# Four output tiles computed together, h tile by h tile, behind each norm; GpSimd taken out of the norms, ScalarE scales the residual

## The chip, the cores and the metric

One core of a Trainium2 chip runs the whole program in one launch. The metric is the device time of that launch in microseconds (us); the kernel before took 3902.36 us, the median of three runs (3899.41 to 3907.14). TensorE (PE) multiplies matrices, VectorE (DVE), ScalarE (ACT) and GpSimd (POOL) work element by element, and SyncE (SP) issues the transfers. Each engine executes its own queue in order and waits at semaphores for the others.

## The reference, cut to what matters

One sequence of 512 tokens with 1024 features passes through a first block (attention and a state-space layer, then a gated FFN, with RMS norms) and then through four layers of a second block. Layer i takes a mixer (0 a conformer convolution module, 1 HGRN2, 2 mLSTM, 3 stick-breaking attention) and then a convolutional FFN. Everything around the change is in these lines:

```
for i in range(4):
    h = x * (1 + scale1) + shift1
    y = mixer_i(h)
    x = layer_norm(ALPHA * x + (1 + gate1) * y, g0, b0)
    h = x * (1 + scale2) + shift2
    y = conv_ffn(h)                  # up: 1024 -> 2 x 2816, conv, silu(gate) * val, down
    x = layer_norm(ALPHA * x + (1 + gate2) * y, g1, b1)
```

A norm needs, for each token, the mean and the mean square over all 1024 features. Two affine copies of the normalized x are used afterwards: h, the input of the next matrix product, and x again as the residual (already multiplied by ALPHA).

## The kernel before

**Layout.** Features lie on partitions: X is eight tiles of 128 features by 512 tokens, and so is h. For precision each float32 operand of a product is split into a high part (a cast to fp32r) and a low part (the difference), so that one 128x128 weight block times one h tile is three matmuls: `mm3` issues L251 (high weight, high h), L254 (low weight, high h) and L255 (high weight, low h). An output tile is a sum over eight h tiles, 24 matmuls into one PSUM bank.

**Weights.** `wload` transfers a block, casts it on ACT (L236) and subtracts on DVE (L237). Four high and four low weight buffers exist, which is just what four output tiles need; a buffer can be cast again once PE's last matmul with it is done.

**Halves.** Around a norm the 512 tokens are worked in two halves of 256 (`HALF`), so that one half can be normalized while PE works on the other. `feats` loops over the halves and in each over four output tiles (`feat`, one bank each, from the four banks of `psm`); `down4` does the last four tiles of a projection in this way. Behind every tile the residual is added on DVE (L624, `add_res`), and `stat` squares the new X on ACT (L343) and adds value and square to running sums on POOL (L356, L358; in the conformer on DVE). With the last tile of a half, float32 matmuls with a matrix of 1/1024 (L348 and L349 for the mean, L351 and L352 for the mean square) give the sums over all partitions in two banks of `psa`.

**The norm.** `ln_scale` forms the variance and its inverse root (ACT L384, three DVE steps L385 to L387 that refine it), subtracts the mean from eight tiles (DVE L399) and multiplies them (L410: six on DVE, tiles 3 and 6, `POOLK`, on POOL). Subtractions 4 to 7 all come ahead of the first multiplication. `ln_apply` then makes hf from X (ACT L444, for tiles 3 and 6 POOL L439), its high part (ACT L244 or L441) and its low part (DVE L247 or POOL L442), and at the end scales X itself for the residual, on POOL (L453), in each half.

**Order.** The Python program is traced in order; a planner then orders each engine's queue by its own estimate of when each instruction can start, earlier program lines first among those that are ready. So a queue need not follow the program, and once the program is built its order is fixed. `tc.add_manual_dep` (`after`) pins an order by hand.

**Where the next stage starts.** Behind the norms stand: the first four up-projection tiles of each FFN (`up` with `jb == 0`, in halves), the first four of HGRN2 (`dense` with `hp == 0`), of mLSTM and of the conformer, and the conformer's own inner norm with `proj_res(early=True)`. The stick layer uses `tok_steps` instead. In the FFN and in mLSTM a tile's bank is read by ACT (L328, `conv_taps`) and by one DVE instruction per tap (L667). In the conformer the first products go through a gate (L1318) into a convolution of 31 taps, done for each of eight tiles partly as DVE steps (L1300) and partly as matmuls (L1294 to L1296).

Of the kernel before, what the change touches and what calls it, by code (L numbers as in the profile page):

```python
# [12 lines left out]
AF = mybir.ActivationFunctionType  # L13
# [17 lines left out]
POOLK = (3, 6)  # L31
# [56 lines left out]
class Kern:  # L88
# [248 lines left out]
    def stat(self, i, v, q, part):  # L337
# [6 lines left out]
        if i == self.ntot - 1:  # L344
# [44 lines left out]

    def ln_scale(self, o, w, X, pool=POOLK):  # L390

# [14 lines left out]
        for k in (4, 5, 6, 7):  # L406
            self.after(sub(k), self.newton)
        for k in range(8):
            e = nc.gpsimd if k in pool else nc.vector
            e.tensor_tensor(out=X[k][:, c], in0=X[k][:, c], in1=y, op=ALU.mult)  # L410
# [14 lines left out]
    def ln_apply(self, gx, bx, gh, bh, parts=HALF):  # L425
# [5 lines left out]
        for o, w in parts:  # L431
            c = slice(o, o + w)
            self.ln_scale(o, w, X, POOLK if gh is not None else ())
            last = None
            for k in range(8) if gh is not None else ():
                hf = self.tmp("hf")[:, :w]
                hi, lo = self.Hh[k][:, c], self.Hl[k][:, c]
                if k in POOLK:
                    nc.gpsimd.tensor_scalar(out=hf, in0=X[k][:, c], scalar1=gh[:, k:k + 1], scalar2=bh[:, k:k + 1],  # L439
                                            op0=ALU.mult, op1=ALU.add)  # L440
                    nc.scalar.copy(out=hi, in_=hf)  # L441
                    last = nc.gpsimd.tensor_tensor(out=lo, in0=hf, in1=hi, op=ALU.subtract)  # L442
                else:
                    nc.scalar.activation(out=hf, in_=X[k][:, c], func=AF.Identity, scale=gh[:, k:k + 1],  # L444
                                         bias=bh[:, k:k + 1])
                    self.split(hf, hi, lo)
            for k in range(8):
                x = X[k][:, c]
                if last is None and k % 2:
                    nc.scalar.activation(out=x, in_=x, func=AF.Identity, scale=gx[:, k:k + 1], bias=bx[:, k:k + 1])  # L450
                    continue
                e = nc.vector if last is None else nc.gpsimd
                i = e.tensor_scalar(out=x, in0=x, scalar1=gx[:, k:k + 1], scalar2=bx[:, k:k + 1], op0=ALU.mult,  # L453
                                            op1=ALU.add)
                if last is not None:
                    self.after(i, last)
# [1678 lines left out]
```

## Time and profile before

| what | value |
|---|---|
| median of three runs | 3902.36 us |
| the profiled execution: own time, span | 3907.43 us, 3905.7 us |
| TensorE clock granted over the span | 0.971 of full |
| busy: PE, DVE, ACT, POOL | 3749.0, 2596.6, 2078.7, 1380.1 us |
| chain that ended last | PE 74%, DVE 11%, POOL 6%, DMA 3%, ACT 3%, issue 2% |
| transferred | 458.06 MB, mean 117 GB/s |

An engine counts as busy while at least one of its instructions runs. The ends of matmuls are modelled and overlap, so that a PE that is only trickling still looks busy; the number of matmuls in a stretch, times the interval at which they start when nothing hinders them, tells how much of the stretch PE needed.

### The profile page before, as it was taken

What the parts mean: (1) busy time and instruction counts of PE and PEld (TensorE: products, weight loads), DVE (VectorE), ACT (ScalarE), POOL (GpSimd) and SP (SyncE); (2) the same over time, 40 slices, a digit from 0 to 9 for tenths busy, and PEclk for the clock granted to TensorE, in tenths of its full rate; (3) what the DMA queues carried; (4) which work ended last, traced back from release to release, by engine and by line L of the source; (5) the groups of instructions that cost most, each with busy time, mean ns of one, the idle gap of its engine ahead of it and who ended that gap; (6) DMA issues with size and microseconds to landing.
All of it is one profiled execution on the core that took longest, in us unless ns stands there. A gap on an engine that the chain in (4) does not pass through costs nothing.

```text
span 3905.7 us, 51250 instructions
## 1 busy us (share of the span) xinstructions
PE 3749.0 (96%) x19014; PEld 3048.5 (78%) x19014; DVE 2596.6 (66%) x3960; ACT 2078.7 (53%) x3757; POOL 1380.1 (35%) x1358
## 2 busy tenths in 40 slices
PE   8999999999996999999999999999899999999998
PEld 7665678878876887898888888776777878788887
DVE  5678866665698765676676567457776566676545
ACT  4555664564644654476465446654556445554333
POOL 5567602343002543342454341255734340022000
PEclk9898899999998999999999999999999999999999
DMA  4111243555321454332245535342255531132231
GB/s 150 54 57 44 69 143 120 190 168 170 108 87 34 157 189 155 122 101 78 99 151 191 166 100 173 133 134 78 74 185 171 173 108 61 46 106 82 93 106 66
DMA packets 393431, 458.06 MB, mean 117 GB/s; under 512 B 35571, under 2 KB 307357, under 8 KB 393181
## 3 DMA queue, kind: packets, MB, share of 16 engines
q1 hardware_dynamic: 393181, 454.78, 35.9%
q8 instruction: 150, 2.46, 0.3%
q14 instruction: 100, 0.82, 0.1%
HBM read 421.56 MB, written 33.03 MB: 116 GB/s over the span
## 4 chain that ended last, share of the span: by engine, by line
PE 74%; DVE 11%; POOL 6%; DMA 3%; ACT 3%; issue 2%; SPq 0%; DVEq 0%; POOLq 0%; ACTq 0%
PE bank L251 20%; PE bank L254 20%; PE bank L255 20%; DMA mix<-in_ada_w_dram 3%; DVE wl L237 2%; PE bank L1906 1%; POOL mix L585 1%; DVE cacc L1300 1%; PE bank L1071 1%; PE bank L1914 1%; ACT mix L583 1%; PE bank L317 1%; PE bank L319 1%; PE bank L318 1%; PE bank L874 1%
## 5 line engine op out<-in xcount | busy, mean ns | idle before, releaser
L251 PE MATMUL bank<-hh,wh 128*128 128x512 f32 (+1 forms) x2928 | 1101.0, 377 | 12.5 <-ACT hh L244 5.3
L254 PE MATMUL bank<-hh,wl 128*128 128x512 f32 (+1 forms) x2928 | 1095.0, 375 | 4.1 <-DVE wl L237 4.1
L255 PE MATMUL bank<-hl,wh 128*128 128x512 f32 (+1 forms) x2928 | 1090.0, 376 | 4.0 <-DVE hl L247 3.4
L237 DVE TENSOR_TENSOR wl<-raw,wh 128x1024 fp32r<-128x1024 f32 (+2 forms) x524 | 668.6, 1277 | 205.9 <-ACT wh L236 199.7
L236 ACT CAST wh<-raw 128x1024 fp32r<-128x1024 f32 (+1 forms) x550 | 562.5, 1026 | 390.9 <-PE bank L255 338.2
L585 POOL TENSOR_TENSOR mix<-mix,mix 128x512 f32<-128x512 f32 x336 | 501.3, 1492 | 757.1 <-ACT mix L583 740.2
L251 PEld LDWEIGHTS bank<-hh,wh 128*128 128x128 f32 x2928 | 557.4, 190 | 126.5 <-ACT hh L244 8.7
L254 PEld LDWEIGHTS bank<-hh,wl 128*128 128x128 f32 x2928 | 556.8, 190 | 111.4 <-DVE wl L237 6.8
L255 PEld LDWEIGHTS bank<-hl,wh 128*128 128x128 f32 x2928 | 551.8, 190 | 114.6 <-DVE hl L247 4.5
L583 ACT ACTIVATE mix<-mix,cs 128x512 f32<-128x512 f32 x384 | 270.6, 722 | 296.9 <-DMA mix<-in_ada_w_dram 295.4
L667 DVE SCALAR_TENSOR_TENSOR mix<-bank,vl,mix 128x510 f32<-128x510 f32 (+3 forms) x384 | 268.6, 700 | 205.2 <-ACT mix L328 197.1
L254 PE MATMUL bank<-uh,wl 128*128 128x512 f32 (+1 forms) x1008 | 371.0, 368 | 3.6 <-DVE wl L237 3.6
L251 PE MATMUL bank<-uh,wh 128*128 128x512 f32 (+1 forms) x1008 | 370.5, 368 | 0.0
L255 PE MATMUL bank<-ul,wh 128*128 128x512 f32 (+1 forms) x1008 | 369.9, 367 | 0.0
L624 DVE SCALAR_TENSOR_TENSOR X<-bank,M,X 128x512 f32<-128x512 f32 (+1 forms) x192 | 120.6, 635 | 238.5 <-PE bank L255 238.2
L254 PEld LDWEIGHTS bank<-uh,wl 128*128 128x128 f32 x1008 | 189.5, 188 | 39.4 <-DVE wl L237 5.4
L251 PEld LDWEIGHTS bank<-uh,wh 128*128 128x128 f32 x1008 | 189.5, 188 | 35.1
L255 PEld LDWEIGHTS bank<-ul,wh 128*128 128x128 f32 x1008 | 189.5, 188 | 34.1
L328 ACT ACTIVATE mix<-bank,vl 128x512 f32<-128x512 f32 (+1 forms) x192 | 141.1, 735 | 86.3 <-PE bank L255 86.2
L244 ACT CAST uh<-mix 128x512 fp32r<-128x512 f32 x110 | 68.0, 618 | 174.3 <-DVE mix L694 173.9
L247 DVE TENSOR_TENSOR ul<-mix,uh 128x512 fp32r<-128x512 f32 x110 | 95.8, 871 | 75.6 <-ACT uh L244 75.1
L358 POOL TENSOR_TENSOR qs<-qs,sq 128x256 f32<-128x256 f32 (+1 forms) x88 | 106.7, 1214 | 54.1 <-ACT sq L343 53.5
(810 smaller groups left out, 7067.1 us busy)
## 6 DMA issues: line engine op xcount, KB each, us to landing
mix<-in_ada_w_dram SPq DMA_DIRECT2D x384, 256.0 KB
raw<-in_ffn_w_up_dram SPq DMA_DIRECT2D x88, 1024.0 KB
raw<-in_ffn_w_down_dram SPq DMA_DIRECT2D x32, 1024.0 KB
raw<-in_w_in_dram SPq DMA_DIRECT2D x22, 1024.0 KB
raw<-in_w_up_dram SPq DMA_DIRECT2D x22, 1024.0 KB
raw<-in_hg_w_in_dram SPq DMA_DIRECT2D x16, 1024.0 KB
raw<-in_ml_w_up_dram SPq DMA_DIRECT2D x16, 1024.0 KB
raw<-in_cc_w_pw_dram SPq DMA_DIRECT2D x12, 1024.0 KB
```

What stands on the lines that cost most here:

```text
L236: nc.scalar.copy(out=h, in_=src)
L237: eng.tensor_tensor(out=l, in0=src, in1=h, op=ALU.subtract)
L247: nc.vector.tensor_tensor(out=lo, in0=src, in1=hi, op=ALU.subtract)
L251: i = mm(out=out, lhsT=wh, rhs=xh, start=start, stop=False)
L254: mm(out=out, lhsT=wl, rhs=xh, start=False, stop=False)
L255: return mm(out=out, lhsT=wh, rhs=xl, start=False, stop=stop)
L328: self.nc.scalar.activation(out=dst[:, o:o + w], in_=ps, func=func, **kw)
L358: self.qadd.tensor_tensor(out=self.qs[:, c], in0=self.qs[:, c], in1=q[:, c], op=ALU.add)
L583: nc.scalar.activation(out=o, in_=o, func=AF.Copy, scale=self.cs[:, k:k + 1])
L585: nc.gpsimd.tensor_tensor(out=acc, in0=acc, in1=o, op=ALU.add)
L624: self.nc.vector.scalar_tensor_tensor(out=x, in0=ps, scalar=gate[:, n:n + 1], in1=x, op0=ALU.mult, op1=ALU.add)
L667: nc.vector.scalar_tensor_tensor(out=d, in0=ps[:, :n - s], scalar=col(s), in1=d, op0=ALU.mult, op1=ALU.add)
```

## The change

`feats` gets `by_k`: four banks are taken at once, the loop over h tiles is outside and the loop over the four output tiles inside, and only then is `use` called for the four. In the second half the banks come from `psa` (banks 4 to 7) if that ring has more than three banks, else from `psm` again (mLSTM). It is used behind the norms, in the conformer's projection, and in the conformer's first block, there with all 512 tokens at a time (before: halves). HGRN2's change of banks moves behind its first `dense`.

`stat` gets `direct`: in the second half of `down4` the last four tiles are not added to the running sums but multiplied by the 1/1024 matrix themselves, one matmul each for value and square as it comes.

In `ln_scale` all multiplications are on DVE, each of tiles 4 to 7 directly behind its subtraction, and `use(k)` follows each; `ln_apply` makes hf on ACT for all eight tiles and scales X on ACT, eight instructions of 512 tokens, behind both halves.

```diff
-    def stat(self, i, v, q, part):
+    def stat(self, i, v, q, part, direct=False):
...
-        if i == self.ntot - 1:
+        if direct:
+            if i == self.ntot - 4:
+                self.st[o] = tuple(self.psa()[:, 0:w] if x else None for x in (self.wmean, True))
+            for ps, t, x in zip(self.st[o], (self.vs if self.wmean else None, self.qs), (v, q)):
+                if ps is None:
+                    continue
+                if i == self.ntot - 4:
+                    mm(out=ps, lhsT=self.smat, rhs=t[:, c], start=True, stop=False)
+                mm(out=ps, lhsT=self.smat, rhs=x[:, c], start=False, stop=i == self.ntot - 1)
+        elif i == self.ntot - 1:
...
-        for k in (4, 5, 6, 7):
-            self.after(sub(k), self.newton)
         for k in range(8):
-            e = nc.gpsimd if k in pool else nc.vector
-            e.tensor_tensor(out=X[k][:, c], in0=X[k][:, c], in1=y, op=ALU.mult)
+            if k >= 4:
+                self.after(sub(k), self.newton)
+            nc.vector.tensor_tensor(out=X[k][:, c], in0=X[k][:, c], in1=y, op=ALU.mult)
+            if use is not None:
+                use(k)
...
-            self.ln_scale(o, w, X, POOLK if gh is not None else ())
...
+            def use(k):
                 hf = self.tmp("hf")[:, :w]
...
+                nc.scalar.activation(out=hf, in_=X[k][:, c], func=AF.Identity, scale=gh[:, k:k + 1], bias=bh[:, k:k + 1])
+                self.set_h(k, c, hf)
+
+            self.ln_scale(o, w, X, use if gh is not None else None)
+        for k in range(8):
+            nc.scalar.activation(out=X[k], in_=X[k], func=AF.Identity, scale=gx[:, k:k + 1], bias=bx[:, k:k + 1])
...
-    def feats(self, tiles, xh, xl, use, halves):
+    def feats(self, tiles, xh, xl, use, halves, by_k=False):
...
-        for parts in (((p,) for p in HALF) if halves else (FULL,)):
+        for p, parts in enumerate(((p,) for p in HALF) if halves else (FULL,)):
+            if by_k:
+                (o, w), = parts
+                get = self.psa if p and len(self.bank["ax"].t) > 3 else self.psm
+                banks = [get()[:, 0:w] for _ in tiles]
+                for k in range(8):
+                    for ps, (blk, j) in zip(banks, tiles):
+                        wh, wl = blk[0][2][j]
+                        self.mm3(ps, wh[:, k, :], wl[:, k, :], xh[k][:, o:o + w], xl[k][:, o:o + w], k == 0, k == 7)
+                for i, ps in enumerate(banks):
+                    use(i, (ps, o, w))
+                continue
...
-            self.stat(*ts[i], part[1:])
+            self.stat(*ts[i], part[1:], direct=part[1] > 0)
...
-        K.feats([(b, jj) for jj in range(2) for b in (bg, ba)], K.Hh, K.Hl, use, jb in (0, 3))
+        K.feats([(b, jj) for jj in range(2) for b in (bg, ba)], K.Hh, K.Hl, use, jb == 3, jb == 0)
```

## Rows read from the trace of the kernel before

**Rows 1.** The page's first part: busy us (share of the span) xinstructions.

```profile
PE 3749.0 (96%) x19014; PEld 3048.5 (78%) x19014; DVE 2596.6 (66%) x3960; ACT 2078.7 (53%) x3757; POOL 1380.1 (35%) x1358
```

**Rows 2.** Stretches: window, us, busy by engine (xcount), clock, DMA share, GB/s; seven norms.

```profile
1262.00:1285.00 23.00, 18.80 (x122) 16.45 (x123) 21.55 (x44) 17.64 (x44) 17.08 (x23) 0.93 0.46 156
1644.00:1668.00 24.00, 21.81 (x145) 19.91 (x144) 23.69 (x55) 14.95 (x33) 19.07 (x25) 0.86 0.30 91
1935.70:1958.00 22.30, 18.19 (x115) 15.63 (x115) 21.54 (x44) 16.47 (x41) 16.69 (x22) 0.90 0.45 154
2314.00:2345.00 31.00, 26.75 (x192) 24.22 (x191) 28.23 (x58) 19.99 (x51) 24.78 (x30) 0.97 0.30 82
2790.00:2815.00 25.00, 20.08 (x132) 18.52 (x131) 24.39 (x50) 18.30 (x41) 22.32 (x23) 0.86 0.38 127
3178.00:3203.00 25.00, 19.93 (x109) 15.77 (x108) 22.78 (x48) 14.78 (x36) 18.95 (x25) 0.86 0.27 85
3505.00:3535.00 30.00, 25.38 (x177) 23.18 (x176) 24.58 (x60) 18.93 (x46) 21.92 (x26) 0.89 0.22 71
```

**Rows 3.** The same view, two stretches inside the third norm.

```profile
1940.00:1945.00 5.00, 4.95 (x25) 4.27 (x25) 4.37 (x9) 4.20 (x12) 1.25 (x2) 0.66 0.24 74
1945.00:1954.00 9.00, 9.00 (x77) 8.97 (x76) 8.94 (x20) 5.08 (x12) 8.82 (x12) 1.00 0.56 201
```

**Rows 4.** The timeline of PE, third norm: start us, us, instruction, [idle before <-releaser].

```profile
1926.01 0.59 PE L349 MATMUL bank<-X,inv 128*128 128x256 f32 x2
1926.56 0.38 PE L352 MATMUL bank<-sq,inv 128*128 128x256 f32 x1
...
1937.82 0.70 PE L348 MATMUL bank<-vs,inv 128*128 128x256 f32 x2 [1.26 <-POOL vs L356]
...
1939.87 0.43 PE L251 MATMUL bank<-hh,wh 128*128 128x256 f32 x1 [0.48 <-ACT hh L244]
...
1941.37 0.41 PE L254 MATMUL bank<-hh,wl 128*128 128x256 f32 x1
...
1955.79 0.38 PE L251 MATMUL bank<-hh,wh 128*128 128x256 f32 x1 [1.47 <-ACT hh L244]
```

**Rows 5.** The timelines of DVE (two rows) and ACT (three rows), third norm.

```profile
1933.78 0.96 DVE L387 SCALAR_TENSOR_TENSOR y<-nb,y 128x256 f32<-128x256 f32 x1
...
1936.38 3.21 DVE L410 TENSOR_TENSOR X<-X,y 128x256 f32<-128x256 f32 x5
...
1937.22 0.60 ACT L444 ACTIVATE hf<-X,lnc 128x256 f32<-128x256 f32 x1 [0.25 <-DVE X L410]
...
1939.41 0.41 ACT L244 CAST hh<-hf 128x256 fp32r<-128x256 f32 x1
...
1941.21 0.40 ACT L244 CAST hh<-hf 128x256 fp32r<-128x256 f32 x1
```

**Rows 6.** Line L410, the multiplications: xcount, ns minimum/median/maximum.

```profile
L410 DVE TENSOR_TENSOR X<-X,y x84: 409/414/1514, 1262.4 to 3525.6; 128x256 f32<-128x256 f32 x84
L410 POOL TENSOR_TENSOR X<-X,y x28: 724/738/987, 1260.8 to 3529.5; 128x256 f32<-128x256 f32 x28
```

**Rows 7.** Who PE waited for from 1278 to 1284 us: total, times, longest.

```profile
PE bank L251 <- DVE mix L667: 1.8, 2, 1.4
```

**Rows 8.** Timelines of ACT (two rows), DVE and PE behind the third norm's four tiles.

```profile
1967.17 1.04 ACT L236 CAST wh<-raw 128x1024 fp32r<-128x1024 f32 x1
1968.11 0.56 ACT L328 ACTIVATE mix<-bank,vl 128x256 f32<-128x256 f32 x1
...
1969.69 1.21 DVE L237 TENSOR_TENSOR wl<-raw,wh 128x1024 fp32r<-128x1024 f32 x1
...
1970.96 0.50 PE L254 MATMUL bank<-hh,wl 128*128 128x512 f32 x1 [0.85 <-DVE wl L237]
```

**Rows 9.** Stretches (columns as in rows 2) of the conformer's convolution.

```profile
1040.00:1160.00 120.00, 120.00 (x687) 105.23 (x686) 110.19 (x165) 76.59 (x188) 0.00 (x0) 1.00 0.25 79
1160.00:1200.00 40.00, 4.98 (x33) 4.82 (x32) 40.00 (x90) 1.68 (x3) 0.00 (x0) 0.57 0.08 27
```

More of the change, by code (lines that the diff above doesn't have):

```diff
@@ L30 @@
 ZEARLY = 20
-POOLK = (3, 6)
 SIG = 5
@@ L388, in rsqrt2, with ln_scale @@
         return y
-    def ln_scale(self, o, w, X, pool=POOLK):
+    def ln_scale(self, o, w, X, use=None):
         nc = self.nc
@@ L432, in ln_apply @@
             c = slice(o, o + w)
-            self.ln_scale(o, w, X, POOLK if gh is not None else ())
-            last = None
-            for k in range(8) if gh is not None else ():
+            def use(k):
                 hf = self.tmp("hf")[:, :w]
[L437 to L456, printed above, removed]
+                nc.scalar.activation(out=hf, in_=X[k][:, c], func=AF.Identity, scale=gh[:, k:k + 1], bias=bh[:, k:k + 1])
[3 more added lines that the diff above has]
+            nc.scalar.activation(out=X[k], in_=X[k], func=AF.Identity, scale=gx[:, k:k + 1], bias=bx[:, k:k + 1])
     def rms_apply(self, g, parts=HALF, log=False):
@@ L696, in use @@
                 self.split(v, *hid[j])
-            self.feats([(b, jj) for jj in range(2) for b in (bg, bv)], self.Hh, self.Hl, use, halves)
+            self.feats([(b, jj) for jj in range(2) for b in (bg, bv)], self.Hh, self.Hl, use, halves, halves)
             if steps is not None:
@@ L761, in use @@
                 self.stat(*ts[i], part[1:])
-            self.feats(tiles, xh, xl, use, early)
+            self.feats(tiles, xh, xl, use, early, early)
 def weave(*gens):
@@ L1385, in dense @@
             K.feats([(b, jj) for b in (bq, bf) for jj in range(2)], K.Hh, K.Hl,
-                    lambda i, part: K.act(qf[i], [part]), True)
+                    lambda i, part: K.act(qf[i], [part]), True, True)
         else:
@@ L1510, in core @@
         yield
-    K.set_banks(mm=(0, 1, 2), ax=(3, 4, 5, 6, 7))
     cur = []
@@ L1515, in hgrn2 @@
         pass
+    K.set_banks(mm=(0, 1, 2), ax=(3, 4, 5, 6, 7))
     for hp in range(4):
@@ L1589, in use @@
             K.conv_taps(part, cw, cb, jb * 2 + i, 4, xc[i], edge[i])
-        K.feats(tiles, K.Hh, K.Hl, use, jb == 0)
+        K.feats(tiles, K.Hh, K.Hl, use, jb == 0, jb == 0)
         if jb == 0:
```

## The prediction, made before the changed kernel ran

> **What bounds the kernel now.** I read the engines' busy time first: PE is busy for 96% of the span, DVE for 66% [rows 1]. PE's own work sets the time, so a change gains only where PE starves, and loses wherever it gives PE more to do. Next come the stretches behind the seven layer norms [rows 2]. The busy figure does not show the starving, so I count matmuls instead. In the third norm, from 1945 to 1954 us, 77 start in 9.00 us at full clock [rows 3]: 0.117 us each. The seven stretches last 180.3 us and hold 122+145+115+192+132+109+177 = 992 matmuls, which need 116.1 us. Eight of them in each stretch are halves of float32 matmuls. A float32 pair costs 0.43 us: from L349 at 1926.01 to L352 at 1926.56 is 0.55 us, and one 0.117 us matmul lies between [rows 4]. That adds about 0.1 us for each half, 5.6 us in all. So 180.3 - 116.1 - 5.6 = 58.6 us are lost, 8.4 us a norm; some records may be missing, so this is an upper figure. It is 1.5% of the kernel and caps the gain.
>
> Then the third norm in detail. PE waits 1.26 us for POOL's sums, 0.48 us for the first h tile and, after the first half's four tiles, 1.47 us for the second half's [rows 4]. From 1940 to 1945 us it runs at a mean granted clock of 0.66 [rows 3], part of the time at the lower level of 1.2 GHz, after those waits. The first h tile is late: its variance is refined at 1933.78 + 0.96 = 1934.74, but its multiplication starts only at 1936.38 behind four subtractions and a residual addition, hf at 1937.22, and the cast ends at 1939.41 + 0.41 = 1939.82 [rows 5].
>
> One thing speaks for caution. Between 1939.87 and 1941.37 PE issues six matmuls, L251 and L254 in turn, while only one h tile has been cast; the second cast ends at 1941.61 [rows 4, 5]. One h tile and one output tile allow only one such pair, so these belong to several output tiles. The planner already goes h tile by h tile where h is late; `by_k` only fixes that order.
>
> **The change part by part.** I work out the third norm and carry it to the others.
>
> *Norm, first half.* With the multiplication directly behind the refinement: 1934.74 + 0.41 [rows 6] + 0.60 + 0.41 [rows 5] = 1936.2, against 1939.82, 3.6 us sooner. PE ends the projection at about 1935.9, then has float32 work. Before it has two of the four pairs ahead of h and gets to h at 1939.87. After, `direct` has ten pairs instead of four, eight of them before the last tile's: 8 x 0.43 = 3.4 us, so PE gets to h at about 1935.9 + 0.4 (two transposes) + 3.4 = 1939.7. The start of h thus hardly moves, but PE comes without idling and h is there. Before, full speed came only at about 1943.6, with 12 matmuls and one pair done since 1939.87, worth 12 x 0.117 + 0.43 = 1.8 us; it is as if dense work had begun at 1941.7. Gain 1.9 to 2.0 us, the six added pairs (2.6 us) paid. Taken for all seven: 13.3 us. Bounds: 1 us each if DVE is late again (7), 3.5 each if the added pairs fall into idle time (24.5).
>
> *DVE and POOL.* Of a norm's sixteen multiplications and sixteen low parts four each were POOL's; on DVE they cost 8 x 0.41 = 3.3 us more. Against it, DVE's multiplications beside POOL's took far longer than 0.414 us: five in 3.21 us, single ones up to 1.514 us [rows 5, 6]. I take the two as even, inside the 1.9.
>
> *Second half.* Its first h tile was waited for by 1.47 us [rows 4]; in the first norm PE waited 1.8 us for L667 to free banks [rows 7], which the banks of `psa` remove. I take 1.5 us a norm, 10.5 us; bounds 0 and 2.3 (16). The conformer's inner norm and the first block's RMS norm have the same two waits in smaller size: 2.6 us for both, estimated from these rows.
>
> *Residual on ACT.* Eight instructions of about twice 0.60 us a norm [rows 5] less overhead, some 6 us, where ACT is busy 16.47 of 22.30 us [rows 2]; they lie beside PE's second half (96 x 0.117 = 11.2 us) and nothing needs the result before the next projection back. Nothing, unless weight casts queue behind them (below).
>
> *Weights.* All four weight pairs are now in use until the second half's last h tile. Before, the first pair came free about one tile sooner, and even so PE waited 0.85 us for the next stage's low weights [rows 8]. Now the first pair is free 9 x 0.117 = 1.05 us before the end, and a cast (1.04) and a subtraction (1.21) follow [rows 8]: PE waits some 1.2 us more than it can use the high part, against 0.85. I add 1.0 us at eight places (two inner or RMS norms, six norms with `by_k`): 8 us. Bounds: 0, and 4.5 us where four read-outs of 0.56 [rows 8] go ahead of the cast (2.2 + 1.04 + 1.21).
>
> *mLSTM* takes its second half's banks from the same four, which must first be read: 2 us, bounds 0 and 5.6 (four tiles in turn at 1.4). *The RMS norm* gets three more float32 pairs: 1.3 us.
>
> *Conformer.* From 1160 to 1200 DVE is busy all 40.00 us and PE 4.98 [rows 9]: there DVE's convolution sets the end. Its first gate needs output tiles 0 and 1. In halves they end 2 x 24 x 0.117 = 5.6 us before the four are done, with `by_k` over 512 tokens 2 x 3 x 0.234 = 1.4 us before. DVE starts 4.2 us later, and two weight subtractions (2.4 us) move behind that. But DVE had 9.8 us idle from 1040 to 1160 [rows 9], part of it waiting for PE, which absorbs some. I take 3 us, bounds 0 and 6.6.
>
> *Sum.* Gains 13.3 + 10.5 + 2.6 = 26.4; costs 8 + 2 + 1.3 + 3 = 14.3; net 12.1 us less than the profiled execution's 3907.43, 3895.3. That execution lies 5.1 us above the median of the runs shown (3902.36), so for the median 3890.
>
> Weighed against the Trainium skill: "TensorE: Matmul & The Clock Gate", section "HAM oscillation — how this bites in real kernels", found no further gain from double-buffered PSUM. By it the second set of banks would give nothing, and the sum would be 1.8 us higher in the norm of [rows 7]; the row shows a wait for banks, and I go by the row.
>
> **The rivals.**
> *The order was there already.* The planner's interleaving [rows 4] makes `by_k` idle, the first half gains nothing net because the added pairs eat what the sooner h gives; gains 13.1 against costs 14.3: 3904, no change. For it: the six matmuls. Against it: the 3.6 us of the chain do not depend on `by_k`.
> *Most of the loss goes.* Each norm keeps 2 us of its 8.4: 7 x 6.4 + 2.6 - 14.3 = 33 us, 3869. For it: clock and waits belong together [rows 3, 4]. Against it: the float32 pairs are real work.
> *Slower: held weights.* At eight places PE waits for weights that could not be cast before the end of the second half, behind four bank read-outs and ACT's residual scaling. It decides above (26.4 - 6.3)/8 = 2.5 us a place; at the upper 4.5 us it is 36 us, net +15.9: 3918. For it: PE waited there before [rows 8]. Against it: high weights come first and ACT can cast ahead of read-outs.
> *Banks cycled.* If alternating four banks brought the lower clock, 192 matmuls a place at twice the interval, 0.117 us more, for eight places would cost 180 us: 4082. The same page, section "A second HAM failure mode: psum-queue depth-cycling", tells of it. Against it: in 1945 to 1954 the granted clock is 1.00 [rows 3], after several tiles had been worked in turn.
>
> **How the numbers follow.** Chances: forecast 0.44 (3882 to 3898 by itself), order already there 0.26, most of the loss goes 0.15, held weights 0.13, banks 0.02. 0.2%, 7.8 us, is what a measurement of this kernel can tell from no change: faster is below 3894.6, slower above 3910.2. Faster: 0.37 of the forecast, 0.15 and 0.03 of the second case, 0.55. Same: 0.07 + 0.20 + 0.01 = 0.28. Slower: 0.03 + 0.12 + 0.02 = 0.17. The range for 8 in 10 reaches from 3866, just below the large gain, to 3911, short of the held weights' upper end.
>
> **What would show it.** Right: behind each norm PE's first matmul with hh follows the projection with less than 1 us idle, the granted clock in such a stretch is above 0.95, no wait for POOL's sums remains in the five norms with `direct`, and L410 on DVE stays near 0.41 us. The weights' step: PE's wait for L237 where the four tiles end, 1 to 2 us. The conformer's: PE's long wait for DVE grows or ends later by 0 to 6.6 us. Wrong: PE idle for h again, because the planner put weight subtractions ahead of h's low parts; or subtraction 7, now late, holding a bank that PE needs first.

## The result, and the profile after

The changed kernel takes 3943.51 us, the median of four runs (3941.2 to 3955.46), against 3902.16 us of the kernel before in the same runs: ratio 1.0112, 95% interval 1.0097 to 1.0127. It is 41.4 us slower, where 12.1 us less was forecast (3890) and the range ended at 3911. The profiled execution took 3941.57 us, its span 3939.9 us. The page after, busy time and the chain that ended last:

```profile
PE 3761.2 (95%) x18984; PEld 3053.6 (78%) x18984; DVE 2579.1 (65%) x4018; ACT 2131.3 (54%) x3844; POOL 1208.6 (31%) x1125
...
PE 70%; DVE 10%; ACT 7%; DMA 5%; POOL 5%; issue 3%; SPq 0%; DVEq 0%; POOLq 0%; ACTq 0%
```

Against [rows 1] PE has 12.2 us more to do, POOL 171 us less, ACT 53 us more; on the chain ACT went from 3% to 7% and DMA from 3% to 5%. Lines are renumbered: mm3 is now L250, L253, L254; the weight's cast L235 and low part L236; h's cast L243 and low part L246; hf L445, the residual's scaling L450, the bank read-outs L327 and L673, the modulation's scaling and sum L577 and L579. What PE waited for over the whole span (us in total, times, longest), first the kernel before, then the changed one:

```profile
PE bank L348 <- POOL vs L356: 10.7, 7, 3.0
...
PE bank L254 <- DVE wl L237: 7.7, 10, 1.5
...
PE bank L251 <- ACT hh L244: 5.3, 7, 1.5
...
PE bank L251 <- ACT hh L441: 1.5, 2, 1.0
```

```profile
PE bank L250 <- ACT wh L235: 13.4, 13, 3.0
...
PE bank L250 <- ACT hh L243: 9.6, 14, 1.8
PE bank L253 <- DVE wl L236: 8.4, 9, 1.5
...
PE bank L356 <- POOL vs L364: 4.0, 2, 3.5
...
PE bank L250 <- DVE xc L673: 3.5, 2, 1.9
...
PE bank L316 <- ACT hh L243: 2.1, 5, 0.7
```

The waits for POOL's sums fell as forecast (3.5 of the 4.0 us left is one wait behind mLSTM, where direct is not used). In their place stand waits for high and low weights (7.7 us before, 21.8 after, 10.1 of these in the first block's feed-forward) and for h's high part (8.2 before, 1.4 of it in the stick layer; 11.7 after, with L316, the same product there). What ends the waits for h shows in the third norm. PE's timeline there, from the end of the projection on:

```profile
1948.50 0.60 PE L351 MATMUL bank<-X,inv 128*128 128x256 f32 x2
1949.08 0.39 PE L250 MATMUL bank<-hh,wh 128*128 128x256 f32 x1
...
1965.46 0.39 PE L250 MATMUL bank<-hh,wh 128*128 128x256 f32 x1 [1.77 <-ACT hh L243]
1967.94 0.39 PE L250 MATMUL bank<-hh,wh 128*128 128x256 f32 x1 [0.80 <-ACT hh L243]
1974.88 0.39 PE L250 MATMUL bank<-hh,wh 128*128 128x256 f32 x1 [0.99 <-ACT hh L243]
...
1979.84 0.50 PE L250 MATMUL bank<-hh,wh 128*128 128x512 f32 x1 [1.24 <-ACT wh L235]
1981.24 0.50 PE L250 MATMUL bank<-hh,wh 128*128 128x512 f32 x1 [0.90 <-ACT wh L235]
```

The first half went as forecast: no wait for sums, and the first product with hh follows the float32 matmuls without a break, where PE waited 1.26 and 0.48 us before [rows 4]. In the second half PE waits 3.56 us for three casts of h, where it waited 1.47 us once [rows 4], and then 2.14 us for the next stage's high weights against 0.85 for its low ones [rows 8]. ACT's timeline says why:

```profile
1961.82 0.60 ACT L445 ACTIVATE hf<-X,lnc 128x256 f32<-128x256 f32 x1
1962.33 0.80 ACT L450 ACTIVATE X<-X,lnc 128x512 f32<-128x512 f32 x1
...
1971.81 0.83 ACT L450 ACTIVATE X<-X,lnc 128x512 f32<-128x512 f32 x1
...
1972.55 1.98 ACT L577 ACTIVATE mix<-mix,cs 128x512 f32<-128x512 f32 x3
1974.40 0.42 ACT L243 CAST hh<-hf 128x256 fp32r<-128x256 f32 x1
```

Of the eight scalings of 0.8 us, seven stand in ACT's queue before the eighth cast of h (1975.42), among hf, read-outs and the modulation's scaling. PE's wait of 0.99 us ends with the cast of 1974.40. The same in stretches (columns as in [rows 2]): the third norm's two halves, then mLSTM's start; last, in the kernel before, the third norm's second half and mLSTM's start, which lie there some 9.5 and 17 to 22 us earlier.

```profile
1930.00:1960.00 30.00, 29.50 (x223) 27.96 (x222) 21.86 (x54) 17.96 (x37) 4.87 (x8) 1.00 0.35 118
1957.00:1979.00 22.00, 17.70 (x141) 16.67 (x139) 13.79 (x32) 20.07 (x42) 10.38 (x7) 1.00 0.26 87
```

```profile
2340.00:2360.00 20.00, 16.16 (x110) 14.63 (x108) 13.62 (x40) 16.09 (x38) 0.00 (x0) 0.91 0.45 141
2360.00:2380.00 20.00, 17.75 (x103) 16.55 (x104) 17.97 (x43) 11.82 (x25) 1.16 (x3) 0.74 0.55 149
```

```profile
1947.50:1969.50 22.00, 20.08 (x153) 19.46 (x152) 17.51 (x32) 15.54 (x34) 21.46 (x26) 0.92 0.28 89
2343.00:2363.00 20.00, 20.00 (x135) 18.88 (x135) 19.18 (x42) 14.22 (x29) 6.09 (x11) 0.92 0.87 256
```

ACT is busy 20.07 of 22.00 us in the second half, against 15.54 before. At mLSTM's start PE waits seven times in 26 us, 6.0 us in all, the granted clock then falls to 0.74, and 103 matmuls start in 20 us where 135 did before, at 0.92.

The largest single piece is elsewhere, in the first block's feed-forward. From the 64th to the 118th cast of wh (some 610 to 920 us) the kernel before takes 297.1 us, the changed one 310.0. SP's timeline there in the changed kernel, and one row of ACT's:

```profile
612.46 37.88 SPq L229 DMA_DIRECT2D raw<-in_w_up_dram  x4
...
675.37 2.56 SPq L229 DMA_DIRECT2D raw<-in_w_up_dram  x2
688.36 6.65 SPq L576 DMA_DIRECT2D mix<-in_ada_w_dram  x4
...
752.64 1.71 SPq L576 DMA_DIRECT2D mix<-in_ada_w_dram  x2
763.49 3.90 SPq L229 DMA_DIRECT2D raw<-in_w_up_dram  x2
```

```profile
768.88 1.05 ACT L235 CAST wh<-raw 128x1024 fp32r<-128x1024 f32 x1 [7.01 <-DMA raw<-in_w_up_dram]
```

### The profile page after: what moved, and what is told of

Read it like the earlier page. It is cut to its first block, busy times and chain, and to the rows that moved or that the text cites. A ratio compares the mean times of both kernels' runs of the same rounds, so it can differ in the third digit from the quotient of the medians.

```text
span 3939.9 us, 51003 instructions
## 1 busy us (share of the span) xinstructions
PE 3761.2 (95%) x18984; PEld 3053.6 (78%) x18984; DVE 2579.1 (65%) x4018; ACT 2131.3 (54%) x3844; POOL 1208.6 (31%) x1125
## 4 chain that ended last, share of the span: by engine, by line
PE 70%; DVE 10%; ACT 7%; DMA 5%; POOL 5%; issue 3%; SPq 0%; DVEq 0%; POOLq 0%; ACTq 0%
PE bank L250 19%; PE bank L253 19%; PE bank L254 19%; DMA mix<-in_ada_w_dram 4%; POOL mix L579 2%; DVE wl L236 2%; ACT mix L577 1%; PE bank L1912 1%; DVE cacc L1306 1%; ACT wh L235 1%; ACT hf L445 1%; PE bank L1920 1%; PE bank L1077 1%; PE bank L880 1%; PE bank L316 1%
## 5 line engine op out<-in xcount | busy, mean ns | idle before, releaser
L250 PE MATMUL bank<-hh,wh 128*128 128x512 f32 (+1 forms) x2896 | 1090.7, 380 | 24.9 <-ACT wh L235 9.9
L253 PE MATMUL bank<-hh,wl 128*128 128x512 f32 (+1 forms) x2896 | 1084.1, 377 | 2.6 <-DVE wl L236 2.4
L254 PE MATMUL bank<-hl,wh 128*128 128x512 f32 (+1 forms) x2896 | 1064.4, 378 | 5.1 <-DVE hl L246 5.0
L236 DVE TENSOR_TENSOR wl<-raw,wh 128x1024 fp32r<-128x1024 f32 (+2 forms) x524 | 668.3, 1277 | 201.6 <-ACT wh L235 200.3
L235 ACT CAST wh<-raw 128x1024 fp32r<-128x1024 f32 (+1 forms) x550 | 562.8, 1026 | 412.5 <-PE bank L254 358.4
L579 POOL TENSOR_TENSOR mix<-mix,mix 128x512 f32<-128x512 f32 x336 | 509.0, 1515 | 789.1 <-ACT mix L577 776.0
L250 PEld LDWEIGHTS bank<-hh,wh 128*128 128x128 f32 x2896 | 549.7, 190 | 145.2 <-ACT hh L243 15.7
L253 PEld LDWEIGHTS bank<-hh,wl 128*128 128x128 f32 x2896 | 549.7, 190 | 111.1 <-DVE wl L236 4.8
L254 PEld LDWEIGHTS bank<-hl,wh 128*128 128x128 f32 x2896 | 537.3, 190 | 117.7 <-DVE hl L246 7.1
L577 ACT ACTIVATE mix<-mix,cs 128x512 f32<-128x512 f32 x384 | 269.7, 722 | 285.8 <-DMA mix<-in_ada_w_dram 284.7
L673 DVE SCALAR_TENSOR_TENSOR mix<-bank,vl,mix 128x510 f32<-128x510 f32 (+3 forms) x384 | 268.9, 702 | 200.1 <-ACT mix L327 188.0
L253 PE MATMUL bank<-uh,wl 128*128 128x512 f32 (+1 forms) x1008 | 372.2, 369 | 5.7 <-DVE wl L236 5.7
L250 PE MATMUL bank<-uh,wh 128*128 128x512 f32 (+1 forms) x1008 | 373.1, 370 | 3.1 <-ACT wh L235 3.0
L254 PE MATMUL bank<-ul,wh 128*128 128x512 f32 (+1 forms) x1008 | 370.9, 368 | 0.0
L253 PEld LDWEIGHTS bank<-uh,wl 128*128 128x128 f32 x1008 | 190.0, 188 | 42.4 <-DVE wl L236 7.9
L250 PEld LDWEIGHTS bank<-uh,wh 128*128 128x128 f32 x1008 | 189.9, 188 | 39.4 <-ACT wh L235 4.0
L254 PEld LDWEIGHTS bank<-ul,wh 128*128 128x128 f32 x1008 | 189.9, 188 | 34.5
L327 ACT ACTIVATE mix<-bank,vl 128x512 f32<-128x512 f32 (+1 forms) x192 | 141.0, 736 | 90.9 <-PE bank L254 90.8
L243 ACT CAST uh<-mix 128x512 fp32r<-128x512 f32 x110 | 67.9, 617 | 168.9 <-DVE mix L700 168.8
L246 DVE TENSOR_TENSOR ul<-mix,uh 128x512 fp32r<-128x512 f32 x110 | 93.9, 853 | 77.8 <-ACT uh L243 77.3
L366 POOL TENSOR_TENSOR qs<-qs,sq 128x256 f32<-128x256 f32 (+1 forms) x70 | 84.4, 1206 | 101.6 <-ACT sq L342 100.7
```

Source lines behind the costliest of these rows:

```text
L235: nc.scalar.copy(out=h, in_=src)
L236: eng.tensor_tensor(out=l, in0=src, in1=h, op=ALU.subtract)
L246: nc.vector.tensor_tensor(out=lo, in0=src, in1=hi, op=ALU.subtract)
L250: i = mm(out=out, lhsT=wh, rhs=xh, start=start, stop=False)
L253: mm(out=out, lhsT=wl, rhs=xh, start=False, stop=False)
L254: return mm(out=out, lhsT=wh, rhs=xl, start=False, stop=stop)
```

## The experiments

All runs in one table. "Above" is the median minus that of the kernel before in the same runs; "rest" is the time from the 64th cast of wh to the end of the span in the profiled execution, which leaves out the attention of the first block, where the program is nearly the same (the kernel before 3286.8, the changed one 3329.8).

| run | median us (runs) | above | ratio, 95% | rest |
|---|---|---|---|---|
| changed kernel | 3943.51 (4) | +41.4 | 1.0112 (1.0097 to 1.0127) | 3329.8 |
| e1 old order | 3923.22 (4) | +18.8 | 1.0046 (1.0031 to 1.0061) | 3309.7 |
| e2 no direct | 3940.74 (4) | +36.3 | 1.0094 (1.0077 to 1.011) | 3318.7 |
| e3 residual on POOL | 3923.94 (4) | +19.5 | 1.0047 (1.0032 to 1.0062) | 3305.9 |
| e4 norms as before | 3925.44 (4) | +21.0 | 1.0047 (1.003 to 1.0063) | 3312.0 |
| e5 = e1 and e3 | 3903.71 (10) | +4.0 | 1.0008 (0.9998 to 1.0018) | 3292.6 |
| e6 = e5, no direct | 3910.59 (10) | +10.8 | 1.0023 (1.0013 to 1.0033) | 3295.6 |
| e7 = e6, order at the norms | 3910.82 (8) | +11.1 | 1.0031 (1.0021 to 1.0042) | 3294.5 |
| e8 old order, first FFN | 3928.13 (4) | +28.4 | 1.0076 (1.0055 to 1.0097) | 3318.8 |
| e9 before + direct | 3893.11 (10) | -5.3 | 0.9983 (0.9973 to 0.9992) | 3280.7 |
| e10 before, norms on DVE | 3902.45 (10) | +4.1 | 1.0013 (1.0002 to 1.0024) | 3285.7 |
| e11 order in first half | 3942.63 (4) | +44.2 | 1.0108 (1.009 to 1.0127) | 3330.7 |
| e12 residual last on ACT | 3930.97 (4) | +32.6 | 1.0079 (1.006 to 1.0099) | 3315.0 |
| e13 e9 + second banks | 3899.76 (11) | -1.3 | 0.9997 (0.9987 to 1.0006) | 3278.9 |
| e16 e13 + order | 3904.17 (11) | +3.1 | 1.0006 (0.9997 to 1.0015) | 3285.6 |
| e14 modulation cut | 3916.34 (4) | +15.3 | 1.0039 (1.0025 to 1.0053) | 3302.1 |
| e15 e14, old order, first FFN | 3918.68 (4) | +17.6 | 1.0042 (1.0027 to 1.0058) | 3299.6 |
| e17 e9 again | 3896.22 (12) | -1.7 | 0.9994 (0.9986 to 1.0003) | 3275.3 |
| e18 e10 + direct | 3895.61 (12) | -2.3 | 0.9992 (0.9982 to 1.0002) | 3278.9 |

**Which part of the change costs.** Four runs undo one part each; three theories were set against each other. "Old order", here and below, is `by_k` False: the output tiles follow one another again and all banks come from `psm`, so that it takes back the order and the second set of banks together.

```diff
 # e1: in feats
+        halves, by_k = halves or by_k, False
 # e2: in down4
-            self.stat(*ts[i], part[1:], direct=part[1] > 0)
+            self.stat(*ts[i], part[1:], direct=False)
 # e3: in ln_apply, where there is an h
-            nc.scalar.activation(out=X[k], in_=X[k], func=AF.Identity, scale=gx[:, k:k + 1], bias=bx[:, k:k + 1])
+            nc.gpsimd.tensor_scalar(out=X[k], in0=X[k], scalar1=gx[:, k:k + 1], scalar2=bx[:, k:k + 1],
+                                    op0=ALU.mult, op1=ALU.add)
 # e4: ln_scale and ln_apply of the kernel before
```

e1: 

> All of the change but the order of the output tiles: every stage goes output tile by output tile again, in halves as before (the conformer's first gate too). Theory W (held weights and banks: four weight pairs stay in use to the end of a stage's second half, so the next stage's casts and low parts come late, and mLSTM waits for banks): PE's idle time at the places with four tiles falls by some 20 us and the time with it, to 3915 to 3925. Theory A (ScalarE's queue: the residual scaling and the additional hf stand among the casts of h): those waits are there in either order, the time stays within 6 us of the changed kernel, 3937 to 3944. Theory F (the float32 matmuls of direct): no change, 3940 to 3944.

e2: 

> All of the change but direct: GpSimd sums the last four tiles of the second half again. 33 float32 matmuls of 0.43 us less are 14.2 us of PE's work. Theory F (they are the loss, nothing of them is hidden): the waits for GpSimd's sums come back by no more than 1 us a norm, the time falls by 9 us or more, to 3934 or below. Theories W and A: the waits for the sums (1.3 to 1.7 us in five norms) and the idle time that the float32 matmuls filled come back and take most of it, within 6 us of the changed kernel: 3937 to 3949.

e3: 

> All of the change, but the residual's scaling runs on GpSimd, on whole tiles of 512 tokens, in the norms that make an h. Theory A: in the second half PE's waits for the casts of h on ScalarE (together 3 to 4.5 us in the first and third norm, 1.5 to 2 in the others) go, and the next stage's weights are cast sooner: 12 to 18 us less, 3925 to 3931. Theory W: the waits for h go but the stage then waits for its successor's weights just as long, within 5 us, 3938 to 3946. Theory F: no change.

e4: 

> All of the change but the norms' division of labour: multiplication, hf, low parts and residual stand on VectorE, ScalarE and GpSimd as in the kernel before; direct, the order by tiles of h and the bank sets are the changed kernel's. Theory A: it gains at least what the residual on GpSimd gains and more, 15 to 25 us less, 3918 to 3928. Theory W: within 6 us of the changed kernel, and slower rather than faster, because VectorE is slowed by GpSimd again: 3940 to 3950.

The order (e1) and the residual on ACT (e3) cost some 20 us each, so theories W and A both hold, for different stretches; F is not borne out by the medians (e2's interval overlaps the changed kernel's; by the rest e2 is 11.1 us faster, so that direct's share stays unclear here). e4 is no better than e3: of the norms' new division of labour, nothing but the residual shows a cost here. The stages tell the two apart. Of the 43.0 us of the rest, 12.9 lie up to the 118th cast of wh (the first block's feed-forward), 5.4 up to the 160th (the conformer), 3.0 up to the 329th, 8.8 up to the 353rd (the norm ahead of mLSTM and its start) and 12.9 behind it. In e3 these are 12.0, 5.4, -0.3, 1.8 and 0.3, in e1 -1.3, 0.8, 5.5, 5.6 and 12.3. The residual's loss lies behind the conformer, the order's in the first block and the conformer. Most of the waits for weights go with the order, those for h with the residual. What PE waited for in e3 and then in e1:

```profile
PE bank L250 <- ACT wh L235: 13.0, 13, 2.8
PE bank L253 <- DVE wl L236: 9.2, 10, 1.9
PE bank L250 <- ACT hh L243: 3.6, 4, 1.1
```

```profile
PE bank L250 <- ACT hh L243: 5.6, 11, 0.9
...
PE bank L253 <- DVE wl L236: 2.9, 6, 0.7
```

**Are the two losses separate, and where is the order's?**

```diff
 # e5: e1 and e3; e6: also direct=False; e7: e3, direct=False, and the old order only where
 # K.byk is False: the first block's feed-forward and the conformer's first gate; e8: the changed
 # kernel, K.byk False in the first block's feed-forward alone
+        if by_k and not self.byk:
+            halves, by_k = True, False
```

e5: 

> The changed kernel with two parts undone at once: output tile by output tile again, and the residual's scaling on GpSimd. Left of the change are direct, the multiplications and low parts on VectorE and the later bank set. If the two losses are separate (by the order 20 us, all of it in the first block and the conformer; by ScalarE's queue 20 us, in the norms and mLSTM), both go: 3901 to 3909, level with the kernel before. If they are one loss seen twice (the same late weights), the time stays above 3912.

e6: 

> As the run with two parts undone, and GpSimd sums the last four tiles again (no direct): left are only the multiplications and low parts on VectorE. If the 14 us of float32 matmuls cost more than the waits that they remove, as the profiles so far say (11 us from the first block's end on), it is 3 to 11 us below the run with two parts undone: 3893 to 3903. If direct pays once the other two are out of the way, it is slower than that run: 3905 to 3912.

e7: 

> As the run with three parts undone, but four output tiles go together behind the seven norms, in HGRN2, mLSTM and the two inner places; only the first block's feed-forward and the conformer's first gate keep the old order. If the order costs by holding the weights in every norm, it is 5 to 15 us slower than the run with three parts undone, 3902 to 3915. If its loss is the first block's and the conformer's alone and it gives nothing behind the norms, within 3 us of that run: 3893 to 3903. If it gains once h is not late on ScalarE, below 3893.

e8: 

> The changed kernel, with the old order in the first block's feed-forward alone. If held weights push the modulation's loads (in_ada_w) behind six weight loads in SyncE's queue there, so that later weight loads stand behind them, some 13 us of the 20 come back here: 3927 to 3934. If the order costs evenly at all its places, 2 to 4 us come back: 3938 to 3943.

They are separate within the noise: both undone, 37.4 of the 41.4 us are back (e5), one by one 22.6 (e1) and 21.9 (e3). e6 missed its expectation: without direct the time is 6.9 us higher, not lower, so direct seems to pay once ACT is out of the way (3.0 us by the rest, and the two intervals overlap). e7 equals e6: behind the norms the order and the second set of banks together neither gain nor cost. Two waits change places. Those for weights are 13.1 us in total against e6's 4.2, which is the size forecast for held weights (8 us); those for a bank's read-out are 1.1 us against 10.1. Two lines of e6, then one of e7:

```profile
PE bank L250 <- DVE mix L681: 5.6, 2, 3.9
...
PE bank L250 <- DVE mix L678: 4.5, 2, 3.4
```

```profile
PE bank L251 <- ACT wh L236: 7.4, 9, 1.2
```

e8 alone brings back 13 us (11.0 by the rest), so most of the order's loss lies in the first block's feed-forward. Of what is left the conformer's first gate has some 4 us: between the 118th and the 160th cast e8 takes 345.3 us, e1 341.2, and e7, with the order in the conformer's projection but not at its gate, 340.8.

**Parts alone, held weights, the queue of ACT.**

```diff
 # e9: the kernel before, with stat's direct branch and direct=part[1] > 0 in down4
 # e10: e6, with the residual per half inside the loop over parts, on gpsimd
 # e11: in feats of the changed kernel
-            if by_k:
+            if by_k and (p == 0 and halves or not halves):
 # e12: ln_apply of the changed kernel; hcast is the last cast of h
+            if gh is not None:
+                self.after(i, self.hcast)
```

e9: 

> The kernel before with direct alone. Direct was worth 7 us where the order was the old one and the residual on GpSimd. If it pays by the waits for GpSimd's sums that it removes, whoever works in the norms: 3890 to 3896. If it needs the norms on VectorE (in the kernel before GpSimd's part of the norm is late anyway): 3897 to 3903, no change. If its 14 us of float32 matmuls are not hidden: above 3905.

e10: 

> The kernel before with the norms' multiplications, hf and low parts on VectorE and ScalarE alone; the residual is scaled by GpSimd half by half as before, the order is the old one and there is no direct (the bank set of HGRN2 alone stays late). With whole residual tiles behind both halves this was 3910.6. If the 11 us above the kernel before are the price of taking GpSimd out of the norms: 3907 to 3913. If they come from the whole tiles being scaled late: 3896 to 3903.

e11: 

> The changed kernel, with four output tiles together in a stage's first half only; in its second half they follow one another (and take their banks from psm), so that the first weight pair comes free about 8 us sooner (72 matmuls of 0.117 us). If held weights are what costs 15 us in the first block's feed-forward, by pushing the modulation's loads and the later weight loads back, most of that goes: 3925 to 3933. If it is the order in the first half, which changes what the planner places before it: 3938 to 3946. In the stage of mLSTM the banks of psa are no longer taken, which would be up to 5 us more.

e12: 

> The changed kernel with the residual's scaling still on ScalarE, but held until the last cast of h. If it costs because it stands among the casts of h in ScalarE's queue: 8 to 20 us back, 3924 to 3936. If it costs because eight instructions of 0.8 us more stand before the read-outs of banks, the weight casts and mLSTM's first stage, wherever they are put: within 5 us of the changed kernel, 3938 to 3950.

e12 brings back 8.8 us by its median and 14.8 by the rest, though its interval just overlaps the changed kernel's: about half of the residual's loss is its place among the casts of h. What the other half is was not tested; the scalings then stand ahead of the next weight casts, and PE waits less for h and longer for weights (e12):

```profile
PE bank L250 <- ACT wh L235: 17.3, 15, 4.0
...
PE bank L250 <- ACT hh L243: 3.3, 4, 1.1
```

e10 says that taking GpSimd out of the norms costs 4 us (interval 1 to 9 us) instead of gaining. e6, with whole residual tiles behind both halves, lies higher still, but the two intervals overlap. e11's time falls in the second of its ranges, but is no clear verdict. In the first block's feed-forward 7.0 of 14.2 us come back (303.0 us from the 64th to the 118th cast, e8 295.8), and elsewhere the second half waits for banks, longest behind the norm that follows mLSTM:

```profile
2842.68 0.55 PE L250 MATMUL bank<-hh,wh 128*128 128x256 f32 x1 [8.75 <-DVE mix L673]
```

**The modulation's loads, and the second set of banks.** SP's timeline of e8 at the same place as the changed kernel's above:

```profile
606.75 1.96 SPq L577 DMA_DIRECT2D mix<-in_ada_w_dram  x3
612.68 0.38 SPq L230 DMA_DIRECT2D raw<-in_w_up_dram  x1
617.02 0.33 SPq L577 DMA_DIRECT2D mix<-in_ada_w_dram  x1
625.67 24.90 SPq L230 DMA_DIRECT2D raw<-in_w_up_dram  x3
...
749.94 7.28 SPq L230 DMA_DIRECT2D raw<-in_w_up_dram  x2
```

With the old order four of the modulation's loads are issued at 606 to 617 us; with the new one they stand behind six weight loads, at 688. From then on the modulation is late and its loads stand between the weight loads: the two of w_up are issued at 749.94 in e8, at 763.49 in the changed kernel, where ACT then waits 7.01 us for them. e14 and e15 cut these loads; in both the modulation is scaled and summed over 32 of 512 columns and its result left out.

```diff
 # e14: the changed kernel; e15: the same and e8's edit
-                self.order(nc.sync.dma_start(out=o, in_=w[k * P:(k + 1) * P, blk * T:(blk + 1) * T]))
+                self.order(nc.sync.dma_start(out=o[:, 0:32], in_=w[k * P:(k + 1) * P, blk * T:blk * T + 32]))
 #      (scaling and sum on o[:, 0:32] and acc[:, 0:32]; M is a copy of the bias)
 # e13: e9's direct and the norms of the kernel before, tiles one after the other, and in feats,
 # in the first FFN too, but not at the first gate; HGRN2's change of banks late
+                get = self.psa if p and len(self.bank["ax"].t) > 3 else self.psm
 # e16: the same with the order by tiles of h (old order, all banks from psm, in the first FFN
 # and first gate)
```

e14: 

> The changed kernel with the modulation's work cut: of each load of in_ada_w (384 of 256 KB) only 32 of 512 columns are fetched, scaled and added, and the modulation is the bias alone. To be read against the next run, which has the same cut and the old order in the first block's feed-forward. If the 15 us that the order costs there come from the modulation's loads being placed later, between the weight loads: at most 5 us above the next run. If they come from the order itself or from held weights: 12 to 18 us above it.

e15: 

> The changed kernel with the same cut of the modulation's loads and work and, in the first block's feed-forward alone, the old order. With the full loads the old order there gave 15.4 us. Displaced loads: at most 5 us below the run with the cut and the new order. The order itself: 12 to 18 us below it.

e13: 

> The kernel before with direct, and in a stage's second half the output tiles, still one after the other, take their banks from psa where that has four. The kernel before with direct alone is at 3893.1. If the waits for banks in the second half (1.7 to 2.0 us in the first and third norm of that run, 0.5 to 0.9 in others) are free to be had by a second set of banks: 3885 to 3891. If what is late there is h anyway: 3891 to 3896.

e16: 

> As the run with the second set of banks, but there the four output tiles go together, tile of h by tile of h (not in the first block's feed-forward and not at the conformer's first gate). If the order gains nothing by itself: within 3 us of that run. If it gains where h is not late on ScalarE: 4 us or more below it. If four weight pairs held to the end cost: 4 us or more above it.

With the loads cut the two orders are equal: 3916.34 and 3918.68, and from the 64th to the 118th cast 296.9 and 295.8 us, where the full loads had 310.0 and 295.8 (changed kernel and e8). So the loss there hangs on the modulation's loads and the work on them, which these runs cut together. Which queue passes the delay on is not told apart: weight loads stand behind these loads on SP, and on ACT, where the scalings stand ahead of weight casts, the wait for these loads from 640 to 900 us is 56.3 us in total (e8 47.3).

The second set of banks is enough to displace the loads, without the order by tiles of h. e13 has the second set in the first FFN with the tiles one after the other, and SP issues there just as in the changed kernel, where e9 issued four of the modulation's loads at 610 to 620 us:

```profile
614.39 37.89 SPq L231 DMA_DIRECT2D raw<-in_w_up_dram  x4
...
675.36 3.29 SPq L231 DMA_DIRECT2D raw<-in_w_up_dram  x2
688.90 5.87 SPq L592 DMA_DIRECT2D mix<-in_ada_w_dram  x4
```

From the 64th to the 118th cast e13 takes 305.2 us, e9 295.8. e11, with the order in the first half and no second set, issues them early (609.87 to 620.21) and still loses 7.2 us against e8, for a reason not followed up. The order in both halves without the second set was not run.

e13's time lies above both ranges expected (the kernel before was 2.7 us slower in its runs than in e9's). Its waits for banks behind the norms are gone but for 0.7 us at mLSTM's (e9 4.6 us), yet it is no faster than e9; PE waits for h and weights instead (e13's waits; 4.6 us of those for weights lie in the first FFN):

```profile
PE bank L255 <- DVE wl L238: 6.3, 8, 1.3
PE bank L252 <- ACT hh L245: 6.3, 6, 1.7
PE bank L252 <- ACT wh L237: 4.2, 2, 3.4
```

That total has the loss in the first FFN in it. Without the stretch from the 64th to the 118th cast the rest of e13 is 2973.7 us, that of e9 2984.9 and of e17, the same kernel as e9, 2979.1. A second set of banks may thus be worth 5 to 11 us behind the norms, where two executions of one kernel differ by 5.8; these runs don't decide it.

e16 is 4.4 us above e13, at the edge of its expectation; the intervals overlap, and no gain by the order shows. As e16 lacks the second set in the first FFN (298.4 us there, 6.8 less than e13), the order's price elsewhere may be larger than 4.4.

**Does any part gain?**

e17: 

> The kernel before with direct alone, once more, in more rounds, to tell whether a part of the change beats the kernel before. If the first figure holds: 3 to 8 us below the kernel before of the same chip (ratio 0.998 to 0.999). If it was chance: within 2 us.

e18: 

> The kernel before with direct, and the norms' multiplications, hf and low parts on VectorE and ScalarE alone; the residual stays on GpSimd half by half, the order is the old one. Without direct this was 4 us above the kernel before. If direct is worth 5 to 7 us here too: level with the kernel before, within 3 us of it. If VectorE alone makes h early enough once the sums are out of the way: 4 us or more below the kernel before with direct alone.

e17 is the same kernel as e9 and e18 is e10 with direct (`direct=part[1] > 0`). e9's interval lies below 1, e17's does not, and its 1.7 us fall in the range for chance: direct alone gains something between nothing and 10 us, and a version that surely beats the kernel before was not found. e18 is level with e17, so with direct the norms on DVE cost nothing more, and 6.4 us less above the kernel before than without direct (e10).

## Why the prediction was wrong, step by step

It was off by 53.5 us. Of these 24.4 lie in two parts that cost 37.4 us (e5) where the forecast had 13 (weights 8, mLSTM 2, conformer 3), and 29.1 in gains that did not come: with the two parts undone it is 4.0 us slower, where the forecast's gains less the RMS norm's pairs were 25.1. The split is rough, for e5 takes back the second set of banks too, which had a part in the 10.5 us forecast for the second half. The 2.6 us of the inner and RMS norms and the 1.3 of the latter's pairs were not measured apart.

- **Residual on ACT** ("Nothing, unless weight casts queue behind them") is the step that failed first. The size of the work was right (56 scalings of 0.82 us, 6.6 us a norm). The forecast set it against ACT's idle time, asked when the result is needed, and thought of weight casts alone as what could queue behind it. In ACT's queue the scalings stand ahead of the casts of h and of read-outs as well (the ACT rows); with them on POOL PE's wait for these casts falls from 9.6 to 3.6 us and that for weight casts hardly (13.4 to 13.0, e3). Price 22 us (e3), 8.8 to 14.8 of it by the place among the casts of h (e12). "Perfetto Trace Analysis" of the Trainium skill, section "Tensor Engine Instruction (MATMUL, LD_WEIGHTS)", calls ACT strictly first in, first out; the rows agree, in which the cast of 1974.40, the end of a wait of 0.99 us, starts only behind a scaling of the residual (0.83) and three of the modulation (1.98).
- **mLSTM** was named, with 2 us for banks. It lost 8.8 us (from the 329th to the 353rd cast of wh 178.0 us, 169.2 before), mostly by the same queue: with the residual on POOL (e3) it takes 171.1 us. The wait for banks is 3.5 us (L673).
- **Weights**, 1.0 us at each of eight places, was right behind the norms in the waits (8.9 us more, e7 against e6). The time did not change there, but the waits for banks fell by 9.0 us in the same pair, so that its price by itself stays open. The 13 us in the first block came in a way that the forecast did not have: the step looked at the casts and not at the loads that are queued with the weights on SP. The rows show SP's loads of weights between loads of in_ada_w, and those wait from 730 to 770 us for POOL's sums (six times, 8.0 us) and for DVE's transposition of a sum (once, 9.1 us); the load of w_up at 763.49 itself waits 9.0 us for the low part of an earlier block (`wl`, DVE). "DMA: Bandwidth & Descriptors" of the Trainium skill, section "Anatomy of one DMA — SWDGE (gpsimd) path", says that "any semaphore wait happens on the issuing sequencer before dispatch"; the trace agrees, in which these waits stand on SP. Why the planner moves the loads when the second half takes other banks stays open.
- **Conformer**, 3 us: some 4 (e8 against e1). Right.
- **Norm, first half, 13.3 us**: right in kind. Waits for sums and idle time ahead of h went and the clock there is 1.00. But direct is worth 0 to 10 us (e9, e17), h made sooner on DVE nothing or a loss (e10, e18), and both together, without the order, between 7 us and nothing (e18). In e9 PE waits 8.1 us less for POOL's sums (3.3 against 11.4), and 33 float32 matmuls of 0.43 us are 14.2 us more work; that these took the place of what was idle is a reading, not shown.
- **Second half, 10.5 us**: did not show. With a second set of banks h and weights are late there instead (e13, e16), but e13's loss of 9.4 us in the first FFN hides what it may gain behind the norms, 5 to 11 us by single executions.
- **Rivals.** "Held weights" named the side and a size of 3918, and even ACT's residual scaling, but ahead of weight casts; the runs show it ahead of the casts of h, and the weights' loss by displaced loads. "The order was there already" has e7 and the first half on its side, but none of the losses. "Banks cycled" is refuted, the clock is 1.00 through the third norm. The Trainium skill, "TensorE: Matmul & The Clock Gate", section "HAM oscillation — how this bites in real kernels", found no further gain from double-buffered PSUM in its kernel. e13's median agrees (1.3 us, ratio 0.9997), but with the loss in its first FFN the run can't tell whether the wait of [rows 7] was worth its 1.8 us.

## What to carry to other kernels

An engine that is idle a quarter of a stretch is not free: ask which instructions stand behind the moved one in its queue. Put behind the last cast of h, the scalings cost some 9 to 15 us less, left on GpSimd some 22 us less. A change of banks in one stage can move loads that have nothing to do with it; look at the transfer queue for what is displaced, and compare stage by stage, for one stage's loss can hide another's gain. A wait that is removed may only make room for the next late input, so take away one wait alone on the chip before summing such gains.

## What was not expected of the hardware

The first 2460 matmuls, up to 534 us in the changed kernel, are the same in the same order on PE, and yet the two profiled executions differ by 8.4 us at their end. Stretches of the kernel before, then of the changed one:

```profile
180.00:230.00 50.00, 47.70 (x227) 34.38 (x227) 34.88 (x52) 23.53 (x59) 22.45 (x27) 0.93 0.22 75
```

```profile
180.00:230.00 50.00, 49.00 (x249) 34.42 (x248) 36.28 (x53) 27.05 (x69) 24.11 (x29) 1.00 0.25 85
```

The granted clock is 0.93 in one and 1.00 in the other. By the 64th cast (618.89 and 610.12 us) 8.8 us have come together, so the spans of two single executions say 34 us where the medians say 41; the rest from that cast says 43.0. And a handful of waits under 2 us at mLSTM's start was followed by 20 us at a granted clock of 0.74, though no wait was long.
